# Router logits taken from the rows before their layer norm, with the gain folded into the router's weights

## The chip, the cores and the metric

The kernel runs on one core of a Trainium2 chip. The metric is the device time of one execution in microseconds, here the median of several runs. The engines named below are TensorE (PE: matmuls and transposes), VectorE (DVE), ScalarE (ACT), GpSimd (POOL) and SyncE (SP, which issues most DMAs). Each engine works through its own list of instructions in a fixed order and waits where an operand is not there yet.

## The reference, cut to what matters

Two layers work on 1024 tokens of 1024 channels in float32. Layer 0 mixes with a state-space scan (SSD), layer 1 with dilated-window attention. Each mixer is followed by a residual layer norm, a mixture of experts (MoE) and a second residual layer norm. The change touches the first layer norm of each layer and the two products of the router:

```python
x = _layer_norm(DEEPNORM_ALPHA * x + mix, ln_g[i, 0], ln_b[i, 0])
ffn = _hierarchical_moe(x, ...)
x = _layer_norm(DEEPNORM_ALPHA * x + ffn, ln_g[i, 1], ln_b[i, 1])

def _layer_norm(x, g, b):
    mu = mean(x); var = mean((x - mu)**2)
    return (x - mu) * rsqrt(var + 1e-5) * g + b

def _hierarchical_moe(x, w_rg, b_rg, w_re, b_re, ...):
    g_logits = x @ w_rg + b_rg          # 4 groups, the best one is taken
    e_logits = x @ w_re + b_re          # 32 experts, the best two of the group
```

With w the 1024 x 36 matrix of both routers, the logits of a row a are ((a - mu) * rstd * g + b) @ w + bias. The same number is (a @ (g w)) * rstd + (-mu * rstd) * sum(g w) + (b @ w + bias), where sums run over channels. The changed kernel computes it in this second form.

## The kernel before, in words

A tile is 128 tokens by 1024 channels, and there are eight of them, 0 to 7. Layer 0's mixer runs until about 845 us of the trace, router 0 and MoE 0 until about 1475 us, layer 1's attention until about 2150 us, then router 1 and MoE 1 until the end.

Inside a mixer, the program is written as generators that a small class (Threads) interleaves: each generator yields a pair (cost, latency) and is taken up again when its latency has passed on the planner's own clock. A scheduler of the framework then lays out each engine's list by its model of the times. So a different latency or a different set of waits moves instructions of other threads too.

When the last product of a tile is added to its residual (the row sums at L632 in layer 0 and at L1580 in layer 1), `done()` or `finish()` calls `layer_norm`. It takes the statistics on DVE (two halves at L191, joined at L193, epsilon added at L194) and the power -1/2 on POOL (L195). For tiles 0 to 3 the rows are then scaled on ACT (L201), multiplied by the gain on DVE (L202) and given the bias on POOL (L203), with -mean*rstd from L200. For tiles 4 to 7 DVE does both in two passes (L197, which needs only the mean, and L198, which needs the power). After `yield 0, 7000` the generator goes on with `Router.tile` (L688 to L715). It writes the normalised tile to two DRAM copies X and S from ACT's queue (L694), transposes it by eight 128 x 128 transposes on PE (L699), copies them from PSUM to `hf` or `qk` (L702 on ACT, L704 on DVE), runs 16 matmuls against the router's weights `rw` (L710), and adds the bias by two small DVE additions (L712 for the groups, L713 for the experts).

Selection is done for tiles 0 to 3, 4 to 6 and 7 in three groups by a long row of small DVE instructions (tensors named r for several tiles and q for a single one), with small matmuls at L775, L777 and L793 in between. The last of these gives the token list (toks, L936), by which POOL gathers rows of X (L996), and the MoE begins on PE with transposes of the gathered rows (L1012).

The router's weights and biases are loaded when a `Router` is made (L663 to L670, on SP's queue). For layer 0 that is at the kernel's start, between the first weight loads of the mixer. For layer 1 it is inside MoE 0, at its step EXTRA = 4, between the loads of expert weights (L972).

## Time and profile before

| | value |
|---|---|
| median of three runs | 2806.02 us (2804.73 to 2807.37) |
| the profiled execution | 2806.4 us, its span 2804.7 us |
| PE busy | 2606.4 us (93%) |
| DVE busy | 1690.6 us (60%) |
| ACT busy | 1266.0 us (45%) |
| POOL busy | 618.3 us (22%) |
| DMA | 647.68 MB, mean 231 GB/s |

The profile gives the times of one execution. "Busy" is the time in which an engine executed instructions. A row of the timeline has the start, the time of the group, engine, line, operation, output and inputs, and, in square brackets, how long the engine sat idle before it and what ended that idle time. A row of a table by windows has, for each engine, busy time and number of instructions, then the clock that TensorE was granted as a share of full speed, the busy share of the DMA engines and GB/s.

### The profile page before, as it was taken

The numbers are of one execution on the slowest core, as the hardware profiler recorded it, in microseconds if no ns is written. First come the engines' busy times: TensorE is split into PE (matmuls) and PEld (weight loads), VectorE is DVE, ScalarE is ACT, GpSimd is POOL, SyncE is SP. The second block draws the span as 40 slices with busy tenths as digits, with TensorE's granted clock in tenths as the row PEclk, the third lists the DMA queues.
The fourth block names the chain that finished last, engine by engine and source line by source line (L and its number), as shares of the span: only waits on it lengthen the run. The fifth ranks groups of instructions, "written<-read, shape, count | busy, mean of one in ns | idle before, by whom it ended". The sixth has DMA issues, their size and how long they took to land. (4 is left out here: it accounts for less than half of the span.)

```text
span 2804.7 us, 40430 instructions
## 1 busy us (share of the span) xinstructions
PE 2606.4 (93%) x14744; PEld 1918.7 (68%) x14744; DVE 1690.6 (60%) x3268; ACT 1266.0 (45%) x2002; POOL 618.3 (22%) x554
## 2 busy tenths in 40 slices
PE   8999999999987989998978999999998899999893
PEld 7778878788874556555647887778887465566562
DVE  5686676897674545545737444555568354456464
ACT  3354442535421544545635444444441254456454
POOL 0054332444351321211111000111112221121102
PEclk9999999999997999999998999999997899999997
DMA  5454543735466899999967332333325799999995
GB/s 148 130 151 136 146 126 105 217 117 154 128 221 224 288 400 383 360 388 378 386 232 275 100 114 76 107 121 105 100 92 205 272 371 385 366 393 390 382 384 180
DMA packets 316415, 647.68 MB, mean 231 GB/s; under 512 B 34172, under 2 KB 202548, under 8 KB 283444
## 3 DMA queue, kind: packets, MB, share of 16 engines
q1 hardware_dynamic: 296660, 594.63, 59.2%
q0 software_dynamic: 14944, 33.64, 5.1%
q10 hardware_dynamic: 4608, 16.78, 1.5%
q8 instruction: 119, 1.95, 0.3%
q14 instruction: 84, 0.69, 0.1%
HBM read 598.15 MB, written 66.19 MB: 237 GB/s over the span
## 5 line engine op out<-in xcount | busy, mean ns | idle before, releaser
L991 DVE TENSOR_TENSOR wl<-wr,wh 128x2048 fp32r<-128x2048 f32 x209 | 477.9, 2291 | 290.8 <-ACT wh L987 227.0
L987 ACT ACTIVATE wh<-wr 128x2048 fp32r<-128x2048 f32 x212 | 405.2, 1916 | 264.6 <-DMA wr<-in_moe_w_down_dram 142.3
L178 DVE TENSOR_TENSOR wl<-wr,wh 128x1024 fp32r<-128x1024 f32 x184 | 238.9, 1299 | 125.3 <-ACT wh L177 121.3
L177 ACT ACTIVATE wh<-wr 128x1024 fp32r<-128x1024 f32 x184 | 194.2, 1055 | 231.0 <-PE mm L184 94.4
L182 PE MATMUL mm<-xth,wh 128*128 128x512 f32 x640 | 255.7, 400 | 1.9 <-DVE carry L392 1.2
L184 PE MATMUL mm<-xth,wl 128*128 128x512 f32 x640 | 255.0, 399 | 0.5 <-DVE wl L178 0.5
L183 PE MATMUL mm<-xtl,wh 128*128 128x512 f32 x640 | 253.4, 396 | 1.9 <-DVE xtl L178 1.9
L182 PE MATMUL mm<-wh,xh 128*128 128x512 f32 (+1 forms) x640 | 248.3, 389 | 0.2 <-ACT xh L177 0.2
L183 PE MATMUL gu<-wl,xh 128*112 128x512 f32 x576 | 228.7, 397 | 17.1 <-DVE wl L991 13.8
L183 PE MATMUL mm<-wl,xh 128*128 128x512 f32 (+1 forms) x640 | 241.5, 378 | 0.0
L184 PE MATMUL mm<-wh,xl 128*128 128x512 f32 (+1 forms) x640 | 239.6, 375 | 0.0
L182 PE MATMUL gu<-wh,xh 128*112 128x512 f32 x576 | 230.8, 401 | 2.0 <-ACT wh L987 2.0
L184 PE MATMUL gu<-wh,xl 128*112 128x512 f32 x576 | 229.5, 398 | 0.0
L1051 PE MATMUL gu<-wr,xh 128*64 128x512 f32 (+1 forms) x784 | 211.4, 599 | 15.2 <-DMA wr<-in_moe_w_up_dram 15.0
L996 POOL DMA_INDIRECT G<-X,pl_toks x44 | 68.5, 1557 | 556.5 <-PE tr L1012 486.2
L1112 POOL DMA_INDIRECT S<-y,pl_toks x56 | 106.3, 1899 | 332.4 <-ACT y L1110 243.7
L1051 PEld LDWEIGHTS gu<-wr,xh 128*64 128x64 f32 (+1 forms) x784 | 70.0, 144 | 141.3 <-issue 107.8
L183 PE MATMUL dn<-wl,hh 128*112 128x512 f32 x288 | 122.4, 425 | 20.0 <-DVE wl L991 20.0
L182 PEld LDWEIGHTS mm<-xth,wh 128*128 128x128 f32 x640 | 121.6, 190 | 28.2 <-issue 1.9
L184 PEld LDWEIGHTS mm<-xth,wl 128*128 128x128 f32 x640 | 121.5, 190 | 27.9 <-issue 1.2
L183 PEld LDWEIGHTS gu<-wl,xh 128*112 128x112 f32 x576 | 101.6, 176 | 56.5 <-DVE wl L991 20.3
L183 PEld LDWEIGHTS mm<-xtl,wh 128*128 128x128 f32 x640 | 121.4, 190 | 27.0 <-DVE xtl L178 2.2
(490 smaller groups left out, 5416.8 us busy)
## 6 DMA issues: line engine op xcount, KB each, us to landing
wr<-in_moe_w_gate_dram SPq DMA_DIRECT2D x126, 1024.0 KB, 20.1
wr<-in_moe_w_down_dram SPq DMA_DIRECT2D x126, 1024.0 KB, 22.3
wr<-in_moe_w_up_dram SPq DMA_DIRECT2D x124, 1024.0 KB, 21.5
wr<-in_ssd_w_in_dram SPq DMA_DIRECT2D x80, 512.0 KB, 3.9
wr<-in_attn_w_qkv_dram SPq DMA_DIRECT2D x72, 512.0 KB, 4.4
E<-csd SPq DMA_DIRECT2D x32, 512.0 KB, 4.4
wr<-in_ssd_w_out_dram SPq DMA_DIRECT2D x32, 512.0 KB, 4.0
xt<-x SPq DMA_DIRECT2D x24, 512.0 KB, 3.9
```

The lines of the kernel that those rows point to most:

```text
L177: return (nc.scalar.activation(hi, src, AF.Copy), (eng or nc.vector).tensor_tensor(lo, src, hi.bitcast(F32), op=ALU.subtract))
L178: (eng or nc.vector).tensor_tensor(lo, src, hi.bitcast(F32), op=ALU.subtract))
L182: nc.tensor.matmul(out, lhsT=sh, rhs=mh, start=first, stop=False)
L183: nc.tensor.matmul(out, lhsT=sh, rhs=ml, start=False, stop=False)
L184: return nc.tensor.matmul(out, lhsT=sl, rhs=mh, start=False, stop=last)
L987: chain("act", lambda: nc.scalar.activation(wh, wr, AF.Copy))
L991: chain("dve", lambda: nc.vector.tensor_tensor(wl, wr, wh.bitcast(F32), op=ALU.subtract), *gate)
L996: return nc.gpsimd.indirect_dma_start(out=g[:r], out_offset=None, in_=rt.X[:, :], in_offset=bass.IndirectOffsetOnAxis(ap=tok, axis=0), bou ...
L1051: i = nc.tensor.matmul(out[c], lhsT=x[k][:, c], rhs=w[z][:, n], start=first, stop=last)
L1112: nc.gpsimd.indirect_dma_start(out=S[:, :], out_offset=bass.IndirectOffsetOnAxis(ap=tok, axis=0), in_=y[:tok.shape[0]], in_offset=None, bo ...
```

## The change

`layer_norm` is split. The new `norm_sums` takes the statistics, the power and -mean*rstd; its small tile has three buffers where it had two. What is left of `layer_norm` applies them. `done()` and `finish()` call `norm_sums`, yield a latency of 2000 (ZLAT) where they yielded 7000, and hand the application of the norm to `Router.tile` as a function. The router transposes the rows as they are before the norm, copies the transposes, and only then applies the norm and writes X and S.

The router's weights are multiplied by the gain once, in `Router.__init__`. That takes two more loads of 128 x 8 single float32 elements (g and b with a channel on each partition), two DVE multiplications of 128 x 288, 16 matmuls against a matrix of ones, which leave the sums over channels of g w and b w on every partition, one copy and one addition. Per tile there are two more small DVE instructions: L730 forms sum * (-mean*rstd) + bias ahead of the matmuls, L737 forms logits * rstd + that.

```diff
-def layer_norm(nc, cm, pool, dst, src, g, b, last=False, eng=None):
+def norm_sums(nc, cm, pool, src):
...
+    nc.vector.scalar_tensor_tensor(mv[:, 2:3], mv[:, 0:1], -1.0, mv[:, 3:4], op0=ALU.mult, op1=ALU.mult)
+    return mv
+
+def layer_norm(nc, mv, dst, src, g, b, last=False, eng=None):
...
         def done(h, c):
             a = acc[h, c]
-            layer_norm(nc, cm, sp, a, a, lng, lnb, h == 1)
-            yield 0, 7000
-            yield from st["emit"](4 * h + c, a, lambda: sp.tile([P, 4, P], F32, name="hf", bufs=2),
+            mv = norm_sums(nc, cm, sp, a)
+            yield 0, ZLAT
+            yield from st["emit"](4 * h + c, a, mv, lambda: layer_norm(nc, mv, a, a, lng, lnb, h == 1), lambda: sp.tile([P, 4, P], F32, name="hf", bufs=2),
...
+        gb = tmp[:, 0:2 * KD].rearrange("p (i k) -> p i k", i=2)
+        for k, src in enumerate((ln_g, ln_b)):
+            nc.sync.dma_start(gb[:, k], dap(src, 0, [[1, P], [P, KD]]))
+        bw = tmp[:, 16:16 + KD * 36].rearrange("p (k n) -> p k n", k=KD)
+        for k, dst in ((1, bw), (0, wr)):
+            nc.vector.tensor_tensor(dst, wr, gb[:, k, :, None].to_broadcast([P, KD, 36]), op=ALU.mult)
+        for i, src in enumerate((wr, bw)):
+            for k in range(KD):
+                nc.tensor.matmul(pt[:, 36 * i:36 * i + 36], lhsT=cm.ones, rhs=src[:, k, :], start=k == 0, stop=k == KD - 1)
+        self.sum = early.tile([P, 36], F32, name=f"rs{layer}", bufs=1)
+        nc.vector.tensor_copy(self.sum, pt[:, 0:36])
+        nc.vector.tensor_tensor(self.bias, self.bias, pt[:, 36:72], op=ALU.add)
...
-    def tile(self, i, a, half, pt, pl):
+    def tile(self, i, a, mv, norm, half, pt, pl):
...
-        for dst in (self.X, self.S):
-            (nc.scalar if self.layer in XACT else nc.sync).dma_start(token_rows(dst, self.runs[i], D), a)
...
             hs.append(h)
+        norm()
+        for dst in (self.X, self.S):
+            (nc.scalar if self.layer in XACT else nc.sync).dma_start(token_rows(dst, self.runs[i], D), a)
         yield 900, 1500
+        to = (self.chosen[:, i, 0:4], slice(0, 4)), (self.lg[:, i, :], slice(4, 36))
+        for t, c in to:
+            nc.vector.scalar_tensor_tensor(t, self.sum[:, c], mv[:, 2:3], self.bias[:, c], op0=ALU.mult, op1=ALU.add)
...
-        nc.vector.tensor_tensor(self.chosen[:, i, 0:4], lg[:, 0:4], self.bias[:, 0:4], op=ALU.add)
-        nc.vector.tensor_tensor(self.lg[:, i, :], lg[:, 4:36], self.bias[:, 4:36], op=ALU.add)
+        for t, c in to:
+            nc.vector.scalar_tensor_tensor(t, lg[:, c], mv[:, 3:4], t, op0=ALU.mult, op1=ALU.add)
```

The change moves instructions well beyond the lines that it edits. Three places matter below. In the rows, the lines of the changed kernel have new numbers: L717 are the transposes (L699 before), L734 the logit matmuls (L710), L639 and L1604 the row sums (L632 and L1580), L192, L194 and L195 the statistics, L197 the product -mean*rstd (L200), L204 and L205 the two DVE passes of the norm (L197 and L198), and L996 the loads of expert weights (L972).

The first place is DVE's list at the end of layer 0, from the row sums of the last tile on. Before (tile 6's logits stand between tile 7's statistics):

```order
960 L632 SCALAR_TENSOR_TENSOR acc<-mm,rstd,acc 128x512 x2
961 L191 BN_STATS ln_st<-acc 128x6
962 L712 TENSOR_TENSOR chosen_234<-sm,rb_230 128x4
963 L713 TENSOR_TENSOR lg_233<-sm,rb_230 128x32
964 L191 BN_STATS ln_st<-acc 128x6
965 L193 BN_AGGR ln_mv<-ln_st 128x2
966 L194 TENSOR_SCALAR ln_mv<-ln_mv 128x1
967 L197 SCALAR_TENSOR_TENSOR acc<-acc,ln_mv,lng 128x1024
968 L712 TENSOR_TENSOR chosen_234<-sm,rb_230 128x4
969 L713 TENSOR_TENSOR lg_233<-sm,rb_230 128x32
970 L198 SCALAR_TENSOR_TENSOR acc<-acc,ln_mv,lnb 128x1024
971 L733 TENSOR_REDUCE r_8536<-chosen_234 128x3
```

Now (from tile 7's row sums, up to its first full pass):

```order
982 L639 SCALAR_TENSOR_TENSOR acc<-mm,rstd,acc 128x512 x2
983 L205 SCALAR_TENSOR_TENSOR acc<-acc,ln_mv,lnb 128x1024
984 L737 SCALAR_TENSOR_TENSOR chosen_259<-sm,ln_mv,chosen_259 128x4
985 L737 SCALAR_TENSOR_TENSOR lg_258<-sm,ln_mv,lg_258 128x32
986 L192 BN_STATS ln_st<-acc 128x6 x2
987 L757 TENSOR_REDUCE r_8581<-chosen_259 128x3
988 L194 BN_AGGR ln_mv<-ln_st 128x2
989 L749 TENSOR_TENSOR r_8583<-chosen_259,r_8581 128x12
990 L835 TENSOR_TENSOR r_8709<-chosen_259,r_8581 128x12
991 L195 TENSOR_SCALAR ln_mv<-ln_mv 128x1
992 L204 SCALAR_TENSOR_TENSOR acc<-acc,ln_mv,lng 128x1024
993 L750 TENSOR_TENSOR r_8583<-r_8583,down 128x12
```

The selection of tiles 4 to 6 (rows on r) now begins between tile 7's statistics, and a full pass of tile 6 (L205) has come in behind tile 7's row sums. Tile 7's own logits (L737) follow ten rows further on, and from there its selection (q) alternates with that of tiles 4 to 6.

The second place is PE's list in layer 1, where tiles 0 to 3 are finished among the last attention products (S, tr, pv). Before:

```order
7581 L1651 MATMUL tr<-ident,s 128x128 x2
7582 L1672 MATMUL pv<-vt,pT 64x64 x4
7583 L699 MATMUL tr<-ident,xt 128x128 x8
7584 L1651 MATMUL tr<-ident,s 128x128 x2
7585 L710 MATMUL mm<-rw_9424,qk 64x36 x8
7586 L1672 MATMUL pv<-vt,pT 64x64 x4
7587 L710 MATMUL mm<-rw_9424,qk 64x36 x8
```

Now:

```order
7566 L1675 MATMUL tr<-ident,s 128x128 x2
7567 L734 MATMUL mm<-rw_9470,qk 64x36 x16
7568 L1675 MATMUL tr<-ident,s 128x128 x2
7569 L183 MATMUL mm<-wh,mt 128x512
7570 L184 MATMUL mm<-wl,mt 128x512
7571 L185 MATMUL mm<-wh,mt 128x512
7572 L183 MATMUL mm<-wh,mt 128x512
```

Twelve matmuls of the output product (L183 to L185, rows 7569 to 7580) now stand between the router's matmuls of one tile and the transposes of the next. Before, they stood ahead of the block.

The third place is SP's list inside MoE 0, where the second router is made. Before:

```order
407 L663 DMA rw_9424<-in_moe_w_router_group_dram 128x8x4
408 L664 DMA rw_9424<-in_moe_w_router_expert_dram 128x8x32
409 L669 DMA rb_9427<-in_moe_b_router_group_dram 128x4
410 L670 DMA rb_9427<-in_moe_b_router_expert_dram 128x32
411 L972 DMA wr<-in_moe_w_down_dram 128x2x1024 x2
```

Now:

```order
407 L670 DMA rw_9470<-in_moe_w_router_group_dram 128x8x4
408 L671 DMA rw_9470<-in_moe_w_router_expert_dram 128x8x32
409 L676 DMA rb_9473<-in_moe_b_router_group_dram 128x4
410 L677 DMA rb_9473<-in_moe_b_router_expert_dram 128x32
411 L681 DMA pre_9430<-in_ln_g_dram 128x8x1
412 L681 DMA pre_9430<-in_ln_b_dram 128x8x1
413 L996 DMA wr<-in_moe_w_down_dram 128x2x1024 x2
```

Two loads of single elements (L681) have come between the router's bias and the expert weights. The same two rows stand at the kernel's start behind the first router's biases, ahead of the gain and bias rows of the norm (lng, lnb) and the mixer's third weight load.

31 lines of the change are left out of this document (16 added, 15 removed).

## The prediction

> **What bounds the kernel now.** I read the page's busy times first, then tables by windows around the four places at which tiles are normalised, then the timelines of PE, DVE and POOL there, and last the DMA issues on SP's queue.
>
> ```profile
> span 2804.7 us, 40430 instructions
> PE 2606.4 (93%) x14744; PEld 1918.7 (68%) x14744; DVE 1690.6 (60%) x3268; ACT 1266.0 (45%) x2002; POOL 618.3 (22%) x554
> ```
>
> PE is busy for all but some 198 us, so the change can only earn time where PE stands still or runs at a lower clock. The windows show two kinds of such places. Those of tiles 0 to 3 in layer 0 and in layer 1:
>
> ```profile
> 500.00:510.00 10.00, 5.96 (x22) 3.06 (x21) 10.00 (x9) 4.90 (x7) 9.20 (x5) 0.86 0.73 246
> 510.00:520.00 10.00, 8.74 (x59) 6.80 (x58) 6.26 (x18) 5.21 (x12) 0.00 (x0) 0.80 0.99 345
> 520.00:530.00 10.00, 10.00 (x91) 8.19 (x89) 10.00 (x20) 7.47 (x15) 0.00 (x0) 1.00 0.89 216
> ...
> 2090.00:2100.00 10.00, 8.45 (x102) 6.40 (x102) 9.97 (x50) 5.94 (x23) 5.26 (x3) 1.00 0.39 155
> 2100.00:2110.00 10.00, 5.37 (x73) 3.92 (x72) 9.80 (x27) 3.95 (x16) 5.29 (x3) 0.73 0.32 125
> 2110.00:2120.00 10.00, 10.00 (x68) 7.86 (x70) 4.32 (x14) 1.44 (x4) 1.04 (x1) 0.59 0.40 142
> ```
>
> After the window stand its length, then the busy time of PE, PE's weight loads, DVE, ACT and POOL, then the granted clock. PE is idle for 4.04 + 1.26 = 5.3 us in the first place and 1.55 + 4.63 = 6.2 us in the second, while DVE is full. The lower clock adds 5.96 x 0.14 + 8.74 x 0.20 = 2.6 us there, and 5.37 x 0.27 + 10 x 0.41 = 5.5 us here. What makes DVE full is the norm (rows of the timelines, each with its start and the time of its group):
>
> ```profile
> 500.60 2.10 DVE L202 TENSOR_TENSOR acc<-acc,lng 128x1024 f32<-128x1024 f32 x1
> ...
> 507.43 2.85 DVE L178 TENSOR_TENSOR wl<-wr,wh 128x1024 fp32r<-128x1024 f32 x1
> ...
> 503.56 5.63 POOL L203 TENSOR_TENSOR acc<-acc,lnb 128x1024 f32<-128x1024 f32 x2
> ...
> 507.65 2.05 PE L550 MATMUL st<-xrd,Bt 128*128 128x512 f32 x2 [1.66 <-DVE H L565]
> ...
> 2103.18 2.23 DVE L1725 TENSOR_TENSOR mx<-mlb,ml 128x8 f32<-128x8 f32 x1
> ...
> 2102.66 2.73 POOL L203 TENSOR_TENSOR xt<-xt,xl 128x1024 f32<-128x1024 f32 x1 [1.21 <-PE pv L1672]
> ...
> 2107.57 1.12 PE L699 MATMUL tr<-ident,xt 128*128 128x128 f32 x4 [4.63 <-DVE pT L1656]
> ```
>
> DVE's gain pass (L202) stands ahead of short instructions that PE wants, and DVE instructions beside POOL's bias pass (L203) are stretched: 2.23 us for 8 elements in each partition. PE meanwhile holds the transposes in its list, and they wait for the whole norm.
>
> The other two places are the ends of the mixers, where nothing is left for PE but the last tiles:
>
> ```profile
> 850.00:860.00 10.00, 6.44 (x53) 5.37 (x54) 9.07 (x69) 1.72 (x5) 3.55 (x2) 0.50 0.88 317
> 860.00:870.00 10.00, 5.93 (x27) 5.34 (x26) 8.17 (x64) 0.21 (x1) 2.32 (x3) 0.50 0.60 246
> ...
> 2160.00:2170.00 10.00, 6.54 (x32) 6.02 (x32) 9.82 (x84) 0.41 (x2) 3.25 (x2) 0.50 1.02 426
> ```
>
> Here DVE sets the pace with the selection, and the MoE starts when the token list is gathered.
>
> **The sum, against the profiled execution's 2806.4 us** (0.4 us above the median). Six terms.
>
> *Tiles 0 to 3, layer 0: -4 us.* The transposes no longer wait for the norm, and by the new order L202 and L203 are spread behind the scan's instructions. The gain is at most what is lost there, 5.3 + 2.6 = 7.9 us. But DVE's work is only moved: the four passes must fit into later windows, and 520 to 530 is full already. If they push the scan there, it is +1. I take half of the upper bound, since PE in 520 to 530 is busy throughout although DVE is full.
>
> *Tiles 0 to 3, layer 1: -3 us.* Upper bound 6.2 + 5.5 = 11.7 us. Twelve matmuls of the output product now stand within the block, and one starts 0.23 us after another:
>
> ```profile
> 2146.05 0.39 PE L183 MATMUL mm<-wl,mt 128*128 128x512 f32 x1
> 2146.28 0.39 PE L184 MATMUL mm<-wh,mt 128*128 128x512 f32 x1
> ```
>
> That is 2.7 us of PE work that can run while DVE catches up. This much I take; DVE remains full from 2090 to 2110, with eight more small instructions, so more would need unstretched passes. Lower bound +1: the logits now keep their PSUM buffer until L737, and that waits for POOL's power, which can stand behind a bias pass of 2.73 us.
>
> *End of layer 0: -1.5 us.*
>
> ```profile
> 844.23 1.41 DVE L632 SCALAR_TENSOR_TENSOR acc<-mm,rstd,acc 128x512 f32<-128x512 f32 x2 [0.64 <-POOL rstd L592]
> ...
> 849.06 1.28 DVE L198 SCALAR_TENSOR_TENSOR acc<-acc,ln_mv,lnb 128x1024 f32<-128x1024 f32 x1 [0.27 <-POOL ln_mv L195]
> ...
> 850.49 1.09 PE L699 MATMUL tr<-ident,acc 128*128 128x128 f32 x4 [2.34 <-DVE r L733]
> ...
> 856.50 0.16 DVE L725 TENSOR_TENSOR q<-chosen,q 128x4 f32<-128x4 f32 x1
> 856.57 0.16 DVE L811 TENSOR_TENSOR q<-chosen,q 128x4 f32<-128x4 f32 x1
> ...
> 861.17 0.16 DVE L729 TENSOR_TENSOR q<-q,q 128x8 f32<-128x8 f32 x1
> 861.36 0.17 DVE L743 SCALAR_TENSOR_TENSOR q<-q,chosen 128x8 f32<-128x8 f32 x1
> ...
> 866.35 0.18 DVE L936 SCALAR_TENSOR_TENSOR toks<-q,acc 128x32 int32<-128x32 f32 x1
> ```
>
> Tile 7's transposes can start after L632 instead of L198, 850.3 - 845.6 = 4.7 us earlier. That doesn't carry through, because DVE is the bound: from L632 to the token list (L936) it takes 22.1 us, of which 18.1 us is the least that its instructions need (each line's shortest distance from start to start). The same sum over the new order is 19.3 us, as one more full pass of tile 6 and the new small ones have come in. So the gain is at most 2.8 us, and if all the present waits stayed it would be a loss of 1.2 us. I take a value towards the gain, since selection rows of q and r now alternate: a row that depends on the one before starts some 0.2 us after it (861.36 after 861.17), an independent one after 0.07 (856.50 to 856.57). The writes of X and S come about 5 us later, but the gather waits for the token list, 16 us behind L198.
>
> *End of layer 1: -3 us.*
>
> ```profile
> 2148.06 0.69 DVE L1580 SCALAR_TENSOR_TENSOR wr<-mm,wr 128x512 f32<-128x512 f32 x1 [0.93 <-PE mm L184]
> ...
> 2154.14 1.06 PE L699 MATMUL tr<-ident,wr 128*128 128x128 f32 x8 [1.00 <-DVE wr L198]
> ...
> 2172.71 0.18 DVE L936 SCALAR_TENSOR_TENSOR toks<-q,acc 128x32 int32<-128x32 f32 x1
> ```
>
> From the last row sum to the token list 24.65 us, 22.2 of it DVE's least; in the new order 151 instructions and 20.4 us stand there in place of 162, as selection of tiles 0 to 3 has moved ahead of the row sum. Bounds -4.3 and 0. Tile 7's transposes, which now begin at 2154.14, can follow on the row sum at 2148.8, so its logits will be there when the selection reaches them, and I take most of it.
>
> *Preparing router 0, at the start: +2.5 us.*
>
> ```profile
> 10.00 2.60 SPq L663 DMA_DIRECT2D rw<-_moe_w_router_group_dram  x1
> ...
> 15.28 0.43 SPq L457 DMA_DIRECT2D lng<-in_ln_g_dram  x1
> ...
> 25.06 1.06 ACT L177 ACTIVATE wh<-wr 128x1024 fp32r<-128x1024 f32 x1 [4.05 <-PE mm L183]
> ...
> 2152.28 0.86 PE L793 MATMUL S<-r,pT 128*128 128x32 f32 x6 [0.62 <-DVE pT L791]
> ```
>
> Sixteen matmuls of 36 columns: nearest are those of 32 in rows of six, 0.86 / 6 = 0.14 us each, together 2.3 us on a PE that has no idle time there (at 25.06 ACT waits for it). The two loads are 1024 runs each, as L663 is, which held the queue for 2.60 us; by it everything behind is 5.2 us later. The third weights were split at 25.06 when PE freed the buffer, not when they arrived, so most of that is hidden. Without this cover PE would wait up to 3.7 us more: bounds +2.3 and +6.
>
> The Trainium skill ("DMA: Bandwidth & Descriptors", rules for kernel authors) says that a transfer without a contiguous last dimension becomes one descriptor per element. By that rule the new loads cost as much as L663 although they move a quarter of its bytes, which speaks against this change; by bytes the sum would be about 1 us lower. I go by L663.
>
> *Preparing router 1, inside MoE 0: +2 us.*
>
> ```profile
> 950.04 3.75 SPq L1359 DMA_DIRECT2D pre<-in_positions_dram  x1
> ...
> 955.00:960.00 5.00, 5.00 (x27) 2.81 (x27) 2.05 (x13) 1.63 (x3) 2.22 (x7) 1.00 0.83 154
> ...
> 960.00:990.00 30.00, 30.00 (x197) 18.17 (x192) 18.14 (x21) 15.43 (x15) 5.57 (x2) 1.00 0.99 362
> ...
> L1012 PE MATMUL tr<-ident,h x48: 221/259/316, 889.9 to 1124.8; 112*128 112x112 f32 x36, 128*128 128x128 f32 x8, 32*128 32x32 f32 x4
> L1012 PE MATMUL tr<-ident,h x48: 221/259/316, 2196.7 to 2428.9; 112*128 112x112 f32 x36, 128*128 128x128 f32 x8, 32*128 32x32 f32 x4
> ```
>
> From there on the MoE is bound by its weights (DMA share 0.99), and seven small loads make a hole: 154 GB/s in place of 362. MoE 1 is the same work without them. Between the same transposes MoE 0 takes 234.9 us and MoE 1 232.2, so the hole costs 2.7 us. Two loads of seven would be +0.8; two that hold the queue like L1359 lose 7.5 x (1 - 154/362) = 4.3 us. PE's 2.3 us for the matmuls lie beside waits for weights. I take +2, bounds 0 and +5.
>
> Sum: -4 - 3 - 1.5 - 3 + 2.5 + 2 = -7.0, thus 2799.4 by the profiled execution, 2799 beside the median. DVE's 48 further instructions, all but four of them small, are at most 0.18 us each as L936 is; those within the four places are in the bounds there, the others lie beside a full PE.
>
> **The rivals.**
>
> *The moved passes come back (no change).* DVE is full where tiles 0 to 3 are finished, and it does the same passes a little later. For it: 520 to 530 is full too. Against it: after 2110 DVE is at 4.32 of 10. Then both first places give about -1 together, the ends -2.5, the preparations +4.5: 2807, within +-4.
>
> *The starvation ends altogether.* If the wait of 4.63 us at 2107.57 falls away, so does the clock of 0.73 and 0.59 behind it; then both places give most of their bounds, -6 and -9, and with the ends at -4.5 and the preparations at +4.5 the sum is -15: 2791. The Trainium skill ("TensorE: Matmul & The Clock Gate", the HAM clock gate) has the clock fall after one idle window of about 3.4 us; by that rule the gap need only be cut by a third for the whole clock loss of layer 1 to vanish. Against it: DVE's rows show 9.97 and 9.80 of 10, so something must still wait.
>
> *The small loads decide, slower.* Place: the queue of SP at 959 and at 15 us. If each load of single elements holds the weights as long as L1359 did and nothing hides it, the preparations cost 5 + 6 = 11 us, and with ends and first places giving together no more than -4 the result is +7: 2813. It decides once the preparations cost more than the four places give: a third split later than 29 us and a hole of 10 us more would do it. Against it: MoE 1's comparison gives the present hole only 2.7 us.
>
> *The order.* That the tiles don't get ahead of their norm is excluded by the new lists: the transposes stand ahead of the passes everywhere.
>
> **How the numbers follow.** Forecast 0.46, at 2799 with its own range 2794 to 2803; no change 0.27; starvation ended 0.13; slower 0.14. The range 2790 to 2810 takes in nearly all of the first rival, half of the second and the lower third of the last. A difference of 0.2% is 5.6 us, about what a measurement of this kernel can tell: faster is two thirds of the forecast, the second of the rivals and little else, 0.46; same 0.39; slower 0.15.
>
> **What would show it.** In the windows 500 to 520 and 2090 to 2110 PE busy should rise by 4 and 3 us in sum, and no DVE instruction of 8 columns should last over 1 us. Tile 7's first transposes should start within 1.5 us of its row sum; the distance from there to the token list should be about 20.6 and 21.7 us. At the start the third split should stay within 3 us of 25, and in MoE 0 the hole should grow by 3 to 6 us while its span grows by about 2. I am wrong if the passes of the norm only push the same waits behind 520 or 2110, or if the distances to the token list stay as they are.

## The result

The changed kernel takes 2845.03 us (median, 2840.77 to 2848.42) against 2805.38 us (2803.15 to 2807.37) for the kernel before in the same comparison: ratio 1.0135, 95% interval 1.0123 to 1.0147. By the ratio it is slower by some 38 us where 7 us less were forecast, and the time lies far outside the range of 2790 to 2810. The busy times on the page of its profile show no new work that could explain this:

```profile
span 2843.4 us, 40615 instructions
PE 2619.1 (92%) x14808; PEld 1928.7 (68%) x14808; DVE 1694.4 (60%) x3316; ACT 1265.1 (44%) x2002; POOL 604.2 (21%) x554
```

PE is busy for 12.7 us more, and the span is 38.7 us longer, so PE stands idle for 26 us more. Where this arises is read by following the same instructions through both traces. The difference in their start times at ten places divides the 38.7 us:

| stretch of the kernel before | longer by | the prediction's term |
|---|---|---|
| 0 to 88 us: start, router 0 prepared | +4.8 | +2.5 |
| 88 to 490: scan and products | +3.0 | 0 |
| 490 to 684: tiles 0 to 3, layer 0 | +15.6 | -4 |
| 684 to 844 (last row sum) | +4.3 | 0 |
| 844 to 866: to the token list, layer 0 | -1.3 | -1.5 |
| 866 to 872: gather of MoE 0 to its first transposes | +8.6 | 0 |
| 872 to 1476: MoE 0, router 1 prepared | +3.8 | +2 |
| 1476 to 2148: attention, tiles 0 to 3 within it | +1.0 | -3 |
| 2148 to 2173: to the token list, layer 1 | -3.1 | -3 |
| 2173 to 2178: gather of MoE 1 to its first transposes | +4.0 | 0 |
| the rest | -2.2 | 0 |

Such a table rests on one execution of each kernel. Kernels below that leave a stretch untouched differ there by up to 2 us, in a few places 3, so no smaller number is given a cause.

### The profile page after: what moved, and what is told of

It is laid out like the page before. It is cut to its first block, busy times and chain, and to the rows that moved or that the text cites. A ratio compares the mean times of both kernels' runs of the same rounds, so it can differ in the third digit from the quotient of the medians.

```text
span 2843.4 us, 40615 instructions
## 1 busy us (share of the span) xinstructions
PE 2619.1 (92%) x14808; PEld 1928.7 (68%) x14808; DVE 1694.4 (60%) x3316; ACT 1265.1 (44%) x2002; POOL 604.2 (21%) x554
## 5 line engine op out<-in xcount | busy, mean ns | idle before, releaser
L179 DVE TENSOR_TENSOR wl<-wr,wh 128x1024 fp32r<-128x1024 f32 x184 | 233.0, 1267 | 128.3 <-ACT wh L178 125.8
L183 PE MATMUL mm<-xth,wh 128*128 128x512 f32 x640 | 259.4, 406 | 3.5 <-ACT wh L178 2.3
L185 PE MATMUL mm<-xth,wl 128*128 128x512 f32 x640 | 257.1, 402 | 0.5 <-DVE wl L179 0.5
L183 PE MATMUL mm<-wh,xh 128*128 128x512 f32 (+1 forms) x640 | 248.0, 388 | 1.2 <-ACT xh L178 1.2
L185 PE MATMUL mm<-wh,xl 128*128 128x512 f32 (+1 forms) x640 | 239.6, 375 | 0.0
L183 PE MATMUL gu<-wh,xh 128*112 128x512 f32 x576 | 230.2, 400 | 0.1
L185 PE MATMUL gu<-wh,xl 128*112 128x512 f32 x576 | 228.9, 397 | 0.0
L1075 PE MATMUL gu<-wr,xh 128*64 128x512 f32 (+1 forms) x784 | 210.8, 600 | 12.7 <-DMA wr<-in_moe_w_up_dram 12.7
L1020 POOL DMA_INDIRECT G<-X,pl_toks x44 | 68.5, 1557 | 583.9 <-PE tr L1036 497.5
L1136 POOL DMA_INDIRECT S<-y,pl_toks x56 | 99.8, 1783 | 320.4 <-ACT y L1134 229.2
L183 PEld LDWEIGHTS mm<-xth,wh 128*128 128x128 f32 x640 | 123.6, 193 | 30.8 <-ACT wh L178 2.7
L185 PEld LDWEIGHTS mm<-xth,wl 128*128 128x128 f32 x640 | 123.1, 192 | 28.5 <-issue 1.2
## 6 DMA issues: line engine op xcount, KB each, us to landing
wr<-in_moe_w_up_dram SPq DMA_DIRECT2D x124, 1024.0 KB, 21.8
```

Of the source, the lines that this page charges most:

```text
L179: (eng or nc.vector).tensor_tensor(lo, src, hi.bitcast(F32), op=ALU.subtract))
L183: nc.tensor.matmul(out, lhsT=sh, rhs=mh, start=first, stop=False)
L185: return nc.tensor.matmul(out, lhsT=sl, rhs=mh, start=False, stop=last)
L1020: return nc.gpsimd.indirect_dma_start(out=g[:r], out_offset=None, in_=rt.X[:, :], in_offset=bass.IndirectOffsetOnAxis(ap=tok, axis=0), bou ...
L1075: i = nc.tensor.matmul(out[c], lhsT=x[k][:, c], rhs=w[z][:, n], start=first, stop=last)
L1136: nc.gpsimd.indirect_dma_start(out=S[:, :], out_offset=bass.IndirectOffsetOnAxis(ap=tok, axis=0), in_=y[:tok.shape[0]], in_offset=None, bo ...
```

## The profile after

First the places where tiles 0 to 3 are finished, in windows moved by 8 and 39 us so that they hold the same work (columns as in the prediction: PE, weight loads, DVE, ACT, POOL, clock, DMA share, GB/s):

```profile
507.80:517.80 10.00, 6.56 (x31) 4.16 (x29) 7.12 (x11) 4.28 (x6) 4.53 (x3) 1.00 0.38 110
517.80:527.80 10.00, 8.28 (x71) 6.68 (x71) 6.30 (x19) 4.34 (x14) 0.55 (x1) 0.83 0.97 283
527.80:537.80 10.00, 6.67 (x44) 5.07 (x45) 7.95 (x14) 8.42 (x16) 1.61 (x1) 0.66 0.36 108
...
2129.00:2139.00 10.00, 9.06 (x100) 7.00 (x98) 9.61 (x37) 5.22 (x17) 3.36 (x2) 1.00 0.28 107
2139.00:2149.00 10.00, 5.66 (x75) 4.06 (x74) 9.45 (x34) 5.40 (x17) 7.02 (x4) 0.95 0.27 107
2149.00:2159.00 10.00, 10.00 (x70) 7.67 (x69) 7.83 (x21) 3.01 (x7) 3.35 (x2) 0.54 0.27 105
```

In layer 0 DVE is no longer full (21.4 us of 30, where the three windows of before sum to 26.3): the passes of the norm did move away. PE is nevertheless idle for 8.5 us instead of 5.3. In layer 1 DVE is no less full than it was, and the clock still falls (0.54 in the last window).

Then the ends of the mixers, from the last row sum (L639, L1604) over tile 7's transposes (L717), the token list (L960) and the gather (L1020) to the first transposes of gathered rows (L1036):

```profile
871.99 1.40 DVE L639 SCALAR_TENSOR_TENSOR acc<-mm,rstd,acc 128x512 f32<-128x512 f32 x2
...
872.84 0.63 PE L717 MATMUL tr<-ident,acc 128*128 128x128 f32 x4 [0.68 <-PE sm L734]
...
892.85 0.19 DVE L960 SCALAR_TENSOR_TENSOR toks<-q,acc 128x32 int32<-128x32 f32 x1
...
897.61 1.17 POOL L1020 DMA_INDIRECT G<-X,toks  x1 [0.93 <-DVE h L928]
...
907.37 1.73 PE L1036 MATMUL tr<-ident,G 112*128 112x112 f32 x8 [10.85 <-DMA G<-X,toks]
...
2188.00 0.69 DVE L1604 SCALAR_TENSOR_TENSOR wr<-mm,wr 128x512 f32<-128x512 f32 x1
...
2209.54 0.19 DVE L960 SCALAR_TENSOR_TENSOR toks<-q,acc 128x32 int32<-128x32 f32 x1
...
2211.45 1.11 POOL L1020 DMA_INDIRECT G<-X,toks  x1 [0.17 <-POOL pl_toks L918]
...
2219.34 1.73 PE L1036 MATMUL tr<-ident,G 112*128 112x112 f32 x8 [7.42 <-DMA G<-X,toks]
```

From row sum to token list it is 20.9 and 21.5 us, as predicted (20.6 and 21.7). But the work goes on only when gathered rows arrive, 14.5 and 9.8 us behind the token list. Before it was 5.9 and 5.8:

```profile
867.42 1.24 POOL L996 DMA_INDIRECT G<-X,toks  x1 [1.72 <-DVE key L840]
...
872.25 1.73 PE L1012 MATMUL tr<-ident,G 112*128 112x112 f32 x8 [2.35 <-DMA G<-X,toks]
...
2173.73 1.10 POOL L996 DMA_INDIRECT G<-X,toks  x1 [3.40 <-DVE pT L791]
...
2178.47 1.73 PE L1012 MATMUL tr<-ident,G 112*128 112x112 f32 x8 [3.36 <-DMA G<-X,toks]
```

## Experiments: new form, latency and preparation taken apart

The change has three parts that can be separated: the new form of a tile (transposes ahead of the norm), the latency ZLAT, and the preparation of the router's weights.

**The latency as it was**, in the changed kernel.

```diff
-ZLAT = 2000
+ZLAT = 7000
```

> The changed kernel with the planner's latency ZLAT back at 7000; nothing else differs from it. In its trace the offset against the kernel before grows from 7.4 to 22.8 us between 505 and 710 us, where the scan of the second half stands among the first four tiles. Theory 1 (the short latency lets the planner lay transposes and logits ahead of scan work that is late on the chip): most of these 15 us go, 2828 to 2834. Rival (the norm behind the copies, or the preparation, re-lays the lists whatever the latency): 2840 to 2850.

Measured: 2839.96 us, ratio 1.0129 (1.0112 to 1.0146). The rival holds: putting the latency back doesn't bring the loss back.

**The preparation alone**, with tiles as before.

```diff
+        gw = early.tile([P, KD, 36], F32, name=f"rx{layer}", bufs=1)
+        ...the loads, products, matmuls and sums of the change, into bw, gw and self.sum
```

> The kernel before plus the preparation alone: the two loads of single elements, the two multiplications, the 16 matmuls, the copy and the addition are done for both layers, into scratch that nobody reads; tiles, norm and latency are as before. Theory 1 (preparation costs 2.8 us at the start, the drift of 6.3 us up to 370 us comes with it since nothing else differs there, and the hole in MoE 0 costs up to 3.8): 2814 to 2819. Rival (only what I had priced, 2.5 + 2; the drift is an accident of the lists): 2808 to 2811.

Measured: 2825.53 us, 1.0076 (1.0059 to 1.0092). That is more than either theory allowed, by the ratio 21 us for work that was priced at 4.5.

**The new form without the preparation.**

```diff
-        ...loads, products and matmuls of the preparation
-        nc.vector.tensor_copy(self.sum, pt[:, 0:36])
+        nc.vector.tensor_copy(self.sum, self.bias)
```

> The changed kernel without the preparation: no loads of g and b, no multiplications, no 16 matmuls; the router uses its raw weights, and its bias in place of the sums (so gain and bias of the norm are left out of the logits). Tiles as in the changed kernel. Theory 1 (the tile's new form costs the 15 us at 505 to 710, 5 us in the last scan tiles and 8.6 us at the gather; preparation the rest): 2829 to 2835. Rival (preparation has shifted the scan against its loads and is behind most of it): 2806 to 2815.

Measured: 2828.28 us, 1.0076 (1.006 to 1.0093), its span 24.9 us above that of before. Form and latency cost 21 us by the ratio, and 25 in the profiled execution, without any preparation. This kernel leaves the norm's gain and bias out of the logits, but it still has the new tile for the sums.

**The change in layer 1 alone.**

```diff
         def done(h, c):
-            mv = norm_sums(nc, cm, sp, a)
-            yield 0, ZLAT
+            layer_norm_old(nc, cm, sp, a, a, lng, lnb, h == 1)
+            yield 0, 7000
...
+        if layer:
             ...the preparation; for layer 0 the old tile
```

> Layer 0 as before (norm first, raw weights, latency 7000), the change in layer 1 alone, with its preparation inside MoE 0. Theory 1 (MoE 0 pays 2 to 4 us for the two loads, layer 1 gains little: in the changed kernel the offset goes from 39.1 to 38.7 over attention, router and MoE 1): 2805 to 2810. Rival (layer 1 gains the 6 us I had forecast once layer 0 is undisturbed): 2799 to 2803.

Measured: 2809.31 us, 1.0014 (1.0005 to 1.0024). So nearly all of the loss is made in layer 0.

**The latency alone, in the kernel before.**

```diff
-            yield 0, 7000
+            yield 0, 2000
```

> The kernel before with one number changed: both latencies 'yield 0, 7000' become 2000, so that the work which follows a tile's norm is handed out earlier; the norm itself, the transposes, the logits and the router's preparation stay as before. Theory (the order of the one PSUM buffer 'sm' decides layer 0's first half: with 2000 the scan's cb matmul of the next chunk comes after the 128x512 matmuls of the selection of tiles 0 to 3, with 7000 ahead of them): PE waits for the scan behind the selection, 8 to 13 us are lost between 500 and 620 us, 2812 to 2819 us. Rival (the loss there is the new form of a tile, its later norm and the stores behind it): 2804 to 2808 us, no step between 500 and 620 us.

Measured: 2819.82 us, 1.0054 (1.0037 to 1.0071). One number, with no other edit, costs 16 us. By the trace 10.7 us arise between 490 and 684 us, and 8.9 us in layer 1 ahead of its tail.

## Experiments: the order of layer 0's first half

Scan, RMS sums, logits and selection share one PSUM buffer, `sm`, in the order in which the program asks for it. In the kernel before, the scan's matmul for its next chunk (cb, L527) comes ahead of the four groups of selection matmuls (L793, the third is shown), and E, which needs cb, is begun at 588.71 (rows of PE and of DVE):

```profile
585.16 0.38 PE L527 MATMUL sm<-CT,BT 128*128 128x128 f32 x2
...
588.71 1.40 DVE L541 TENSOR_TENSOR E<-E,cb 128x1024 f32<-128x1024 f32 x1
...
602.04 0.97 PE L793 MATMUL sm<-r,roc 128*128 128x32 f32 x8
```

In the changed kernel all four groups of the selection (L817, the last is shown) stand ahead of it. DVE waits for cb, and PE then waits for DVE:

```profile
609.30 0.98 PE L817 MATMUL sm<-r,roc 128*128 128x32 f32 x8
...
615.17 0.29 DVE L539 TENSOR_TENSOR cb<-sm,triu 128x128 f32<-128x128 f32 x1 [2.52 <-PE sm L534]
616.58 1.42 DVE L548 TENSOR_TENSOR E<-E,cb 128x1024 f32<-128x1024 f32 x1
...
618.05 1.10 PE L565 MATMUL yd<-E,xr 128*64 128x128 f32 x16 [0.52 <-DVE E L548]
623.19 1.11 PE L532 MATMUL tr<-ident,xs 128*128 128x128 f32 x4 [4.05 <-DVE xr L536]
```

The kernel before with 2000 shows the same, with tiles in their old form:

```profile
598.39 0.97 PE L793 MATMUL sm<-r,roc 128*128 128x32 f32 x8
603.86 0.39 PE L527 MATMUL sm<-CT,BT 128*128 128x128 f32 x2
...
607.81 1.09 PE L558 MATMUL yd<-E,xr 128*64 128x128 f32 x16 [2.78 <-DVE E L541]
612.16 1.11 PE L525 MATMUL tr<-ident,xs 128*128 128x128 f32 x4 [3.25 <-DVE xr L529]
```

Two tests followed, on top of two edits that were made for layer 0's gather (next section). In the first, cb comes ahead of the selection again:

```diff
-        yield 1700, 6000
+        yield 1700, 12000 if (self.layer, i) == (0, 3) else 6000
```

> The kernel of c2_no_new_bytes with the latency behind the logits of tile 3 in layer 0 set to 12000 instead of 6000, so that the scan's cb matmul takes the PSUM buffer 'sm' ahead of the selection of tiles 0 to 3, as in the kernel before; nothing else differs. Theory (the order of that buffer costs layer 0's first half 8 to 13 us): the step between 500 and 620 us shrinks to 0 to 5 us and the time is 2824 to 2831 us. Rival (the step is the late norm's own, whatever the order): within 2 us of c2_no_new_bytes.

Measured: 2825.74 us, 1.0076 (1.0053 to 1.0098), within the theory's range, though the interval overlaps that of c2_no_new_bytes (1.0078 to 1.0119). By the traces c2_no_new_bytes is 14.8 us further behind the kernel before at the last row sum of layer 0 than at 490 us, and c5_cb_first 8.7 us. In the second test the selection no longer shares its buffer with cb but with the scan's last product (yd), once with the new form of a tile and once in the kernel before with 2000.

```diff
-AG = "sm"
+AG = "yd"
```

> The kernel of c2_no_new_bytes with one word changed: the selection of layer 0 takes its PSUM tiles from the buffer of the scan's last product (yd) instead of from 'sm', which the scan's first product (cb), the RMS sums and the logits share. Theory (waiting for that shared buffer is what the new order costs): PE's waits of about 4 us on E and xr between 520 and 620 us go, the loss between 490 and 680 us falls from 12 us to 0 to 6 us, 2817 to 2824 us. Rival (the wait only moves to yd, or the order costs by other ways): within 3 us of c2_no_new_bytes.

> The kernel of e5_before_2000 (old form of the tile, latency 2000) with the same word changed: the selection of layer 0 takes its PSUM tiles from the buffer of the scan's last product instead of from 'sm'. Theory (the shared buffer): layer 0 loses nothing against the kernel before, its tail keeps 1.5 us less, layer 1's loss of 9 us ahead of the tail stays: 2807 to 2813 us. Rival: within 3 us of e5_before_2000, 2817 to 2823 us.

Measured: 2825.04 us, 1.0075 (1.0063 to 1.0088), and 2821.46 us, 1.0067 (1.0054 to 1.008), the last against 1.0054 for the kernel without that word. Both rivals hold by the trace (c6_own_buffer is 4.6 us below c2_no_new_bytes, with overlapping intervals): the wait has moved to yd. In c6_own_buffer E is ready early, but the scan's yd product now stands behind all four groups of the selection. In the changed kernel the same product began at 576.68. The state H, the next step of the scan, is then late (604.31 in the kernel before):

```profile
578.37 1.23 DVE L549 TENSOR_TENSOR E<-E,cb 128x1024 f32<-128x1024 f32 x1
...
603.99 0.98 PE L818 MATMUL yd<-r,roc 128*128 128x32 f32 x8
...
610.68 1.09 PE L566 MATMUL yd<-E,xr 128*64 128x128 f32 x16
...
623.40 0.67 DVE L573 TENSOR_TENSOR H<-H,st 128x512 f32<-128x512 f32 x1
```

So these two kernels don't show what the loss would be without sharing; a selection with a buffer of its own wasn't run.

What distinguishes the kernels is seen when the stretch is cut in three at the same weight splits (490, 558, 604, 620 us of the kernel before). The numbers are microseconds lost between them:

| kernel | form, latency | 490 to 558 | 558 to 604 | 604 to 620 | 620 to 684 |
|---|---|---|---|---|---|
| the change | new, 2000 | +8.2 | -3.5 | +7.7 | +3.3 |
| e3_no_prep | new, 2000 | +7.0 | -3.8 | +9.8 | +0.4 |
| e1_zlat7000 | new, 7000 | +13.9 | -3.1 | +0.9 | -3.0 |
| c5_cb_first | new, 2000, cb first | +6.1 | +0.2 | -2.8 | +7.5 |
| c6_own_buffer | new, 2000, selection in yd | +7.9 | -5.2 | +7.1 | +1.1 |
| e5_before_2000 | old, 2000 | +1.6 | -1.9 | +11.4 | -0.3 |
| e8_own_buffer | old, 2000, selection in yd | +1.0 | -4.8 | +11.4 | -1.0 |
| e4_layer1_only | old, 7000 | +0.3 | +0.2 | -0.1 | -0.2 |

There are two separate losses. The one behind 604 us belongs to the order that latency 2000 makes. It goes where cb comes first (c5_cb_first, e1_zlat7000) and comes with the old form too. c5_cb_first and e1_zlat7000 also hand out other work later, so that cb's place alone decides it is a reading of the waits above. In c5_cb_first most of it returns at 680 us, where PE, about to make an RMS sum, waits 4.62 us for POOL's squares. The other, between 515 and 540 us of the changed kernel, belongs to the new form at either latency:

```profile
531.13 1.97 PE L565 MATMUL yd<-E,xr 128*64 128x128 f32 x16 [4.19 <-DVE E L548]
```

Both kernels run the same number of the mixer's products (L183 to L185) ahead of the logits that start at 512.31 before and at 518.67 now. Before, 45 more of them stand between these logits and this matmul's counterpart at 526.92, which doesn't wait. Now 19 stand there, the other 26 have gone behind it, and PE waits for E with the clock at 0.83 and then 0.66. E itself is begun 7.5 us later than before (529.85 for 522.37), no more than the whole stretch, which began 7.8 us later. In the other six kernels with the new form in layer 0, 19 to 28 products stand there, and PE waits 2.1 to 4.0 us in all but e1_zlat7000, whose 13.9 us in this stretch have another source, which isn't located. In the kernels with the old form it is 31 or 45, and PE doesn't wait. What in the new form makes this order wasn't tried apart.

## Experiments: the gather of MoE 0

Two instructions ahead of the gather were new in their waits, though the change touches neither. The first expert-weight load of a row of seven is issued at 877.34, and the list's clearing on POOL (L918) waits for the selection's matmuls (timelines of SP's queue and of POOL, then a window):

```profile
877.34 0.33 SPq L996 DMA_DIRECT2D pre<-in_moe_w_gate_dram  x1
...
896.58 0.10 POOL L918 MEMSET pl_toks<- 64x6 int32 x1 [13.43 <-PE sm L817]
```

```profile
897.00:902.00 5.00, 0.00 (x0) 0.00 (x0) 0.00 (x0) 0.00 (x0) 3.48 (x4) 0.50 1.01 418
```

While rows are gathered, DMA is full with weights. In the kernel before these loads had been issued between 821 and 858 us, and DMA was down to a share of 0.29:

```profile
867.00:872.00 5.00, 2.62 (x12) 2.35 (x11) 1.57 (x9) 0.00 (x0) 3.67 (x4) 0.50 0.29 67
```

The suspicion was the place of two tiles in SBUF. The preparation's scratch takes the first turn of the ring `hf`, and the sums are a new tile of 144 bytes; both move the tiles allocated later onto others, for whose last reader they then wait. The first kernel takes the scratch from the ring `cv_t`, and the second also puts the sums within an older tile.

```diff
-            st["emit"] = router(cp, sp.tile([P, 4, P], F32, name="hf", bufs=2)...
+            st["emit"] = router(cp, sp.tile([P, 4, P], F32, name="cv_t", bufs=2)...
```

> The changed kernel with the preparation's scratch of layer 0 taken from the ring of the convolution's temporaries instead of from the ring that the transposed rows use later, so that the first expert-weight loads no longer wait for the last logit matmuls of layer 0. Theory (those seven loads, issued 20 to 30 us later than before, run beside the gather of MoE 0 and make it slow): the loads are issued by 860 us, the gather takes 5 us from its issue to the first transposes instead of 10, 2838 to 2842 us. Rival (the gather is late by POOL alone and the time is given back later): 2843 to 2846 us.

```diff
-        both = cp.tile([P, 16, 2], F32, name="dboth", bufs=1)
+        dboth = st["rs"] = cp.tile([P, 36], F32, name="dboth", bufs=1)
+        both = dboth[:, 0:32].rearrange("p (a b) -> p a b", b=2)
...
-        self.sum = early.tile([P, 36], F32, name=f"rs{layer}", bufs=1)
+        self.sum = rs if rs is not None else early.tile(...)
```

> The kernel of c1_other_scratch, and the column sums of the weights lie within an older tile instead of a new one of 144 bytes, so that the tiles allocated later stand where they stand in the kernel before. Theory (the list's clearing on POOL, ahead of the gather, waits for the selection's matmuls because the new tile moved it onto the gates' place): the clearing no longer waits for TensorE, the gather is issued another 2 to 4 us earlier, 2835 to 2840 us. Rival (POOL's wait is hidden behind the list's own store): the same as c1_other_scratch within 1 us.

Measured: 2835.22 us, 1.0106 (1.0085 to 1.0127), and 2829.65 us, 1.0099 (1.0078 to 1.0119). The times lie below what both theories had forecast, and the interval of c1 overlaps that of the change a little. From token list to first transposes the traces of the kernel before, of the change, of c1 and of c2 give 5.9, 14.5, 9.2 and 7.3 us. In c1 the gather itself is fast again (4.4 us from its issue) but is issued as late; in c2 the clearing is off the path as well, but the gather takes 6.2 us:

```profile
892.56 0.10 POOL L918 MEMSET pl_toks<- 64x6 int32 x1 [13.41 <-PE sm L817]
...
898.00 1.73 PE L1036 MATMUL tr<-ident,G 112*128 112x112 f32 x8 [5.50 <-DMA G<-X,toks]
```

```profile
880.56 0.10 POOL L919 MEMSET pl_toks<- 64x6 int32 x1 [6.74 <-DVE q L808]
884.16 1.17 POOL L1021 DMA_INDIRECT G<-X,toks  x1 [3.50 <-DVE roc L816]
```

By the trace both theories hold as to what the two instructions wait for. The step from c1 to c2 is not resolved by the times, whose intervals overlap. Nor is the gather mended for good: in c5_cb_first and c6_own_buffer, which have both edits, it takes 8.8 and 8.1 us from its issue. What it goes with is the DMA share. Of the 40 first gathers in the 20 traces, the 18 with a share of 0.88 or more in the 4 us from the issue took 6.2 to 9.8 us, and the 22 with 0.26 to 0.71 took 4.3 to 5.2, three of them 6.1 or 6.2.

## Experiments: the preparation

The preparation without these side effects (scratch and sums as in c2, tiles as before, results unused):

> The kernel before plus the preparation of both routers, as in e2_prep_only (its results are not used, the tiles keep their old form), but without its side effects: the scratch of layer 0 comes from the ring of the convolution's temporaries, both products use one place one after the other, and the sums lie within an older tile. Theory (the preparation itself costs what was predicted, 2.5 us at the start and 2 us in MoE 0; the rest of e2_prep_only came from where its tiles lie): 2807 to 2811 us, the gather of MoE 0 as fast as before. Rival (loads and matmuls of the preparation cost it): 2815 to 2821 us.

Measured: 2815.09 us, 1.0047 (1.0031 to 1.0062), where the rival lies. Side effects were thus some 8 us of e2_prep_only's 21, yet 13 us remain. Four kernels split them: all of router 0's preparation, its loads alone, its products and matmuls alone (ones set by POOL in place of the loaded values), and router 1's alone.

```diff
+        if not layer:        # or: if layer
+            ...the loads, or the products and matmuls, or both
```

> The kernel before plus the preparation of router 0 alone, in place as in p1_prep_in_place and unused; nothing for router 1. Theory (the preparation at the start costs more than the 2.5 us predicted, since it holds up the first products): 2809 to 2813 us. Rival (MoE 0 pays, the start hides it): 2803 to 2806 us.

> The kernel before plus the two loads of single elements for router 0 alone, without products, matmuls or sums. Theory (the loads hold SP's queue, so that every first weight load behind them is 5 us later): most of what q0_prep_layer0 costs, at least 4 us. Rival (the weights are waited for by PE's buffers, not by the queue): 0 to 2 us above the kernel before.

> The kernel before plus the products and the 16 matmuls for router 0 alone, with ones set by POOL in place of the loaded gain and bias, so without the two loads. Theory (the loads are what costs): 2 to 3 us above the kernel before, the matmuls' own time on PE. Rival (the products and matmuls stand in PE's list ahead of the mixer's and wait there): most of what q0_prep_layer0 costs.

> The kernel before plus the preparation of router 1 alone, in MoE 0, unused; nothing for router 0. Theory (it costs the 2 us predicted): 2803 to 2806 us. Rival (its loads and matmuls leave the MoE short of weights): 2809 to 2813 us.

| kernel | median | ratio (95%) |
|---|---|---|
| q0_prep_layer0 | 2813.91 | 1.0029 (1.0017 to 1.0042) |
| q1_loads_layer0 | 2805.96 | 1.0006 (0.9997 to 1.0015) |
| q2_products_layer0 | 2815.44 | 1.0041 (1.0028 to 1.0055) |
| q3_prep_layer1 | 2809.05 | 1.0017 (1.0008 to 1.0026) |

The loads cost nothing that can be measured, and the products and matmuls cost as much as the whole (the intervals of q0 and q2 overlap). The rows of the changed kernel show why they were priced too low (the third is an ordinary product right behind them, and the fourth and fifth stand in MoE 0):

```profile
25.21 1.87 PE L687 MATMUL tr<-rw,ones 128*128 128x36 f32 x16
26.91 2.30 PE L687 MATMUL tr<-hf,ones 128*128 128x36 f32 x16
...
29.59 0.63 PE L184 MATMUL mm<-xtl,wh 128*128 128x512 f32 x1
...
1008.18 1.98 PE L687 MATMUL tr<-rw,ones 128*128 128x36 f32 x16
1009.99 2.35 PE L687 MATMUL tr<-pre,ones 128*128 128x36 f32 x16
```

Eight matmuls of the program are sixteen pieces in the trace. The kernel before shows the same: its 128 logit matmuls of layer 0 are 256 in the trace. The 32 pieces took some 4 us of a full PE at the start (25.21 to 29.21), and the products behind them ran at 0.63 us each instead of 0.39 for some 2 us. There the granted clock was 0.50, though PE shows no idle time (windows of the changed kernel and of the kernel before):

```profile
29.00:31.00 2.00, 2.00 (x6) 1.61 (x7) 1.97 (x4) 0.03 (x1) 0.00 (x0) 0.50 0.37 91
```

```profile
29.00:31.00 2.00, 2.00 (x11) 1.08 (x10) 1.89 (x4) 1.93 (x3) 0.00 (x0) 1.00 0.80 229
```

In the windows of 2 us from 27 to 33 the clock was 0.84, 0.50 and 0.81, which loses 1.7 us; before it was 1.00 in all three. Matmuls and clock together cover the 4.8 us of the first row of the first table. In e2_prep_only the clock falls to 0.50 in the same window. In p1_prep_in_place and q2_products_layer0, where the two sets of sixteen pieces stand apart, it stays at 1.00 from 25 to 40 us.

The two loads that were priced by L663 held SP's queue for 0.43 and 0.58 us:

```profile
15.98 0.43 SPq L681 DMA_DIRECT2D hf<-in_ln_g_dram  x1
16.45 0.58 SPq L681 DMA_DIRECT2D hf<-in_ln_b_dram  x1
```

That is not all of their price on the queue. The next row (lng) held it for 2.55 us instead of 0.43, and the third weight load of the mixer was issued at 20.15 instead of 16.23; 0.7 of these 3.9 us arose ahead of the two loads. The third split then waited for its weights and started at 27.31 instead of 25.06, while PE stayed busy. In q1_loads_layer0 the two loads stand behind lng, lnb and two weight loads, and they held the queue for 4.92 and 1.84 us. That they cost nothing is measured there; for their place in the changed kernel it is read from PE's busy time.

In q3_prep_layer1 PE also waits for the second product of the preparation, behind which the MoE's own matmuls stand:

```profile
977.40 3.63 PE L680 MATMUL tr<-pre,ones 128*128 128x36 f32 x16 [3.69 <-DVE pre L678]
```

This wait doesn't explain router 1's 5 us, however. In that execution the kernel is 5.2 us behind the kernel before at 1000 us and 1.3 us at 1100: before, PE was idle for 5.5 us between 1000 and 1040 with a DMA share of 1.02, and here it is not idle there. Where router 1's 5 us by the ratio arise isn't shown. PE's time for the matmuls is 4 us of router 0's 8 to 11. The remainder isn't located: the profiled execution of q2_products_layer0 has +3.4 us at 88 us and between 4 and 7 us from there to 800.

## Experiments: the end of layer 1, and a version that might beat both

If a lower latency shortens the tails and only tiles 0 to 3 pay for it, tiles 4 to 7 alone could have it. The norm stays where it was. The second kernel also moves half of a clearing behind the first gathers, and the third does only that.

```diff
-            yield 0, 7000
+            yield 0, 2000 if i >= 4 else 7000
```

> The kernel before with the latency 2000 in place of 7000 for tiles 4 to 7 alone, in both layers; form of the tile, its norm and the order of the one PSUM buffer 'sm' in tiles 0 to 3 are those of the kernel before. Theory (the shorter distance from the last row sum to the token list comes from the order in which the selection is handed out, not from transposing ahead of the norm): the distance is 20.5 to 21.3 us in layer 0 (22.1 before) and 21 to 23 us in layer 1 (24.65 before), no step between 500 and 700 us, 2800 to 2804 us. Rival (the moved norm shortens it): both distances as before, 2804 to 2807 us.

```diff
-        for i in (0, 2):
-            nc.gpsimd.memset(pair(i), 0.0)
+        zero = [pair(i) for i in (0, 2)]
+        nc.gpsimd.memset(zero[0], 0.0)
...
         gathers(2)
+        with behind(tc, *first):
+            nc.gpsimd.memset(zero[1], 0.0)
```

> The kernel of b1_late_tiles_2000, and the clearing of the second pair of gather buffers on POOL stands behind the first two gathers instead of ahead of them. Theory (in layer 1 the clearing, which waits for the last store of the normalised rows, is late by then, so that the gather starts together with the weight loads and takes 8 us instead of 4.8): the gather is issued within 1.2 us of the token list and takes about 5 us, 1 to 4 us less than b1_late_tiles_2000. Rival (the gather is slow by chance or is hidden): the same as b1_late_tiles_2000 within 1 us.

> The kernel before with nothing but the clearing of the second pair of gather buffers moved behind the first two gathers. Theory (in the kernel before the clearing is done 3.4 us ahead of the token list, so moving it changes nothing): 2803 to 2806 us. Rival (the clearing behind the gathers delays the third gather and MoE's second block): 2806 to 2809 us.

Measured: 2805.43 us, 1.0013 (1.0004 to 1.0022); 2807.28 us, 1.0016 (1.0007 to 1.0025); 2802.61 us, 0.9999 (0.999 to 1.0008). None beats the kernel before; the interval of k0 takes in 1. The time of b1 is its rival's, and its distance to the token list is 21.6 us in layer 0 and 23.1 in layer 1, between the two theories. In b2 the gather takes 7.5 us from its issue where the theory had about 5. What these kernels bear on is the gather of MoE 1. In the table a gain in the tail comes back behind the token list (microseconds against the kernel before):

| kernel | row sum to token list, layer 1 | token list to first transposes |
|---|---|---|
| the change | -3.1 | +4.0 |
| e1_zlat7000 | -2.0 | +4.3 |
| e4_layer1_only | -4.1 | +4.4 |
| e5_before_2000 | -3.9 | +4.0 |
| b1_late_tiles_2000 | -1.5 | +3.4 |
| b2_late_and_clear | -1.1 | +2.7 |
| e2_prep_only | +0.5 | +1.4 |
| q0_prep_layer0 | +0.1 | +1.5 |
| p1_prep_in_place | +0.3 | -0.4 |
| k0_clear_late | 0.0 | 0.0 |

Windows of the changed kernel and of the kernel before, each from about the issue of the gather, show what it meets, an expert-weight prefetch that has not yet drained (DMA share 1.00 against 0.69):

```profile
2211.00:2215.00 4.00, 0.93 (x5) 0.79 (x4) 0.55 (x4) 0.00 (x0) 3.22 (x5) 0.50 1.00 413
```

```profile
2174.00:2178.00 4.00, 1.11 (x6) 0.97 (x5) 0.70 (x5) 0.00 (x0) 3.08 (x4) 0.50 0.69 208
```

In the change 0.9 of the 4.0 us is a later issue (1.91 us behind the token list for 1.02). The clearing isn't what makes the gather slow: in b1 it is issued 1.02 us behind the token list, as before, and takes 8.1 us. Nor does a gain in the tail account for all, as e2_prep_only and q0_prep_layer0 reach the transposes 1.4 and 1.5 us later without one. That an earlier gather is slow because of that prefetch is read from the windows. A kernel with a later prefetch wasn't run.

## Why the prediction was wrong, point by point

*What bounds the kernel.* Right in that PE lost time around the norms, wrong in the cause for layer 0. DVE was taken for the bound because it was full. With the passes gone DVE has slack, and PE waits longer than before (8.5 us for 5.3). By the waits above, the scan's chain of short steps decides there, and how products are strewn between them.

*Tiles 0 to 3, layer 0: -4, measured +15.6.* This step failed, and with the gather it makes most of the error. The working put the worst case at +1, "if they push the scan there", because it followed only the moved passes. The new order was at hand, and in it the scan's cb had gone behind the selection. The single buffer between them, and what waits for cb, were left out of account. The order that latency 2000 makes costs 10.7 us in this stretch without any new form (e5_before_2000), and in the changed kernel 7.7 us between 604 and 620. The new form adds a loss of its own, 8.2 us between 490 and 558, where 26 products have gone behind the matmul that waits for E; why the new form orders them so stays open.

*Tiles 0 to 3, layer 1: -3, measured +1.0.* PE's idle time in the three windows falls from 6.2 to 5.3 us and the loss by the clock from 5.5 to 4.9, so 1.5 us are gained there and lost elsewhere in the stretch. The longest wait for the transposes was cut as the change meant to, from 4.63 to 2.52 us:

```profile
2147.36 0.66 PE L717 MATMUL tr<-ident,xt 128*128 128x128 f32 x4 [2.52 <-DVE pT L1680]
```

The clock fell to 0.54 in the next window all the same. By the rule that the prediction took from the Trainium skill ("TensorE: Matmul & The Clock Gate", the HAM clock gate), a gap below 3.4 us should have kept it, and the trace doesn't bear that out. The old form at the same latency (e5_before_2000) loses 8.9 us in this stretch, so the new form is worth 8 us here, against a price that the latency itself had set. What the latency costs there was not traced further.

*End of layer 0: -1.5, measured -1.3.* The size is right, its reason is not shown, and that they met is luck as far as the runs go. From tile 7's second row sum to the token list it is 21.4 us before and 20.2 in the change, in c1 and in c2. With the new form at 7000 it is 22.2, with the old form at 2000 20.6, and 21.8 in e3_no_prep, which has the new form and 2000. p1_prep_in_place, whose tiles are as before, has 20.9. Transposing ahead of the norm thus doesn't shorten it by itself, and which part of the order does isn't shown.

*End of layer 1: -3, measured -3.1.* Here both parts shorten it (-2.0 with the new form at 7000, -3.9 with the old at 2000), but they don't add up (-4.1 with both in e4_layer1_only). The step that failed is the one not taken: the term was counted up to the token list, and the gather behind it gave back 4.0 us.

*Preparing router 0: +2.5, and router 1: +2.* The mechanism was right as far as it went, PE's own time for the matmuls. The term was mis-sized: the 0.14 us are those of a piece, so 16 matmuls made 2.3 us where they are 32 pieces and some 4 us, and the clock of 0.50 behind them was not counted. Alone the two preparations cost about 8 and 5 us by the ratios (13 together in p1_prep_in_place), of which only the matmuls' own time is located. The loads were taken by L663 at 2.60 us each. What stands behind them was 3.9 us later where 5.2 had been expected, and that most of it is hidden was right. The Trainium skill's rule of one descriptor per element ("DMA: Bandwidth & Descriptors", rules for kernel authors) had been read as speaking against this change. By these runs the price is there on the queue, but PE doesn't wait for it.

*What was not in the sum.* The gather of MoE 0, +8.6 us. The prediction wrote that the gather waits for the token list. It also waits for what precedes it on POOL, and it shares DMA with loads whose start hangs on where tiles lie in SBUF. The 3.0 us between 88 and 490 and the 4.3 us ahead of the last row sum were not in the sum either, and no run here locates them.

*The rivals.* "The moved passes come back" and "the starvation ends" both took DVE for the cause and fell with it. "The small loads decide" named the right side, the preparations, but the wrong thing in them, by q1_loads_layer0 and q2_products_layer0. "The order" was dismissed because the transposes had moved ahead of the norm everywhere, which is only one part of the order. The rival that was needed is the same one with its object turned round: what else the new order had moved.

*What would show it.* Tile 7's transposes start within 1.5 us of its row sum, at 872.84 in layer 0 and at 2188.40 in layer 1, and both distances to the token list are as forecast. The third split at 27.31 is within 3 us of 25, and MoE 0 takes 236.3 us between the transposes that were named, 1.4 more than before. But PE's busy time in the two places didn't rise as foretold, and these were the tests of the main terms. DVE instructions of 8 columns still last over 1 us (2.29 at 2130.20 and 2.01 at 2144.88).

## What to carry to other kernels

When an edit changes a latency or a wait that a scheduler reads, compare the new lists for everything that shares a single buffer there, and follow each step that has moved behind another to who waits for it; here one number reordered the scan and cost more than all the work that was saved. Count a gain at the end of a stage only up to the first use of its result by the next stage, with the queue that this use shares. A new tile of 144 bytes or a scratch tile from a ring used later can put waits on instructions far away, so look for changed waits on instructions that the edit doesn't touch.
